# When the four weight sums of a seven-product block are formed: together, or one with each product

## The chip, the cores and the metric

The kernel runs on one core of one Trainium2 chip. Its time is the device time in microseconds (us) of one execution; of several runs the median counts. One more execution was profiled: it gives the trace and the profile page that the text reads.

## The reference

One layer of a streaming encoder on 2048 tokens with 1024 features: chunked softmax attention with a relative bias, then a SwiGLU feed-forward, each between two RMS norms and with a residual.

```python
h = rms_norm(x, g_pre_mix)
q, k, v = split_heads(h, w_qkv)             # 16 heads of 64
# chunk c of 64 frames reads chunks c-8 .. c
p = softmax(q @ k.T / 8 + bias)
x = x + rms_norm(merge_heads(p @ v) @ w_o, g_post_mix)
h = rms_norm(x, g_pre_ffn)
x = x + rms_norm((silu(h @ w_gate) * (h @ w_up)) @ w_down, g_post_ffn)
```

All in float32; the inner width of the feed-forward is 2816.

## The kernel before

**Matmuls.** Every float32 operand of a dense product is split into a high part (a rounded copy, made by ScalarE) and a low part (the rest, a subtraction on VectorE). A product is three matmuls, high by high, high by low, low by high: lines 199, 200 and 201 in `products`. A weight block of 128 x 1024 is split by `split_part`, ScalarE on line 131 and VectorE on line 132.

**Seven products for eight.** The large dense layers (values, queries and keys, gate and up, down) work on 2 x 2 blocks with seven block products in place of eight. Both sides need sums for that. On the token side `Blocks.build` makes the operands B11, B21, T1, T2, B22, T3 and T4 (the names in `BLOCKS`, in the order of use): line 741 makes the difference for T1, line 720 the three combinations for each slice of T2, line 691 or 357 (ScalarE) the high part and line 692 or 358 (VectorE) the low part. On the weight side the seven factors are A11, A12, S1, S2, S4, S3 and A22, where S1 = A21 + A22, S2 = A11 + S1, S4 = A12 + S2 and S3 = A11 - A22 in the kernel's signs and storage.

**Where the weight sums are made.** The down weights' sums are made by DMA. Those of the others are made once, in the first of the two token groups of 1024 tokens, by `block_items`: four blocks are loaded, each sum is one VectorE instruction of 128 x 1024 (line 902), written over one of the four blocks, and stored to DRAM by a GpSimd-issued DMA (line 903) for the second group. There are 17 such sets: 2 for the values (v), 4 for queries and keys (q), 11 for gate and up (g), 68 sums in all.

**Order of the work.** `Stream` runs the weight items ahead of their use: when a product is taken, the item three products on is made (`make`: split, then sums), and its loads start up to six ahead. So in the middle of a set the sums of the next one are made. The two v sets alternate item by item, and each v name has two weight tiles. In `make`, before the change, with n the name of the item:

```python
if n == ("B11" if early else "B21"):
    sum_("S1", "A21", "A21", "A22")
    sum_("S2", "A11", "A11", "A21")
if n == "B21":
    sum_("S4", "A12", "A12", "A11")
if n == "T2":
    sum_("S3", "A21", "A11", "A22", ALU.subtract)
```

`early` holds for q and g. TensorE's order is that of the program; the order on VectorE, ScalarE, GpSimd and SyncE is set by a scheduler that goes by readiness and by place in the program. All queues run in order.

**Who reads the banks.** In a q or g set a product is 24 matmuls into two PSUM banks, 12 each. T4 adds to the two banks that T3 filled, after VectorE has read each of them (the closing: line 1289 in q, 1009 in g). In the v stage a product is 48 matmuls; VectorE adds pairs of products on line 1225, and ScalarE scales the values on line 429.

**Beside the v stage.** The row sums of squares come from token-major copies of x, loaded one after the other into one buffer and squared on ScalarE (line 1344); after four of them VectorE (line 1348) and GpSimd (line 1349) make the roots that line 429 needs.

Of the kernel before, what the change touches and what calls it, by code (L numbers as in the profile page):

```python
# [13 lines left out]
ALU = mybir.AluOpType  # L14
# [24 lines left out]
BLOCKS = ("B11", "B21", "T1", "T2", "B22", "T3", "T4")  # L39
# [10 lines left out]
def trunk(  # L50
# [74 lines left out]
    def w_tile(name):  # L125

        t = wp.tile([P, 2, 1024], F32R, tag="w", name=f"w_{name}", bufs=4)
        return Parts(t)

    def split_part(hi, lo, raw):  # L130
        act.activation(hi, raw, AF.Copy)  # L131
        dve.tensor_tensor(lo, raw, hi.bitcast(F32), op=ALU.subtract)  # L132
# [694 lines left out]
    def weight_sums():  # L827

        def long(t):
            return t.rearrange("(a b) c -> a (b c)", b=2)

        def copy(to, a):
            with tc.issue_after(last_sp[0].ins):
                last_sp[0] = nc.sync.dma_start(long(to), long(a), max_dma_last_dim=8192)

        def add(to, a):
            with tc.issue_after(last_pool[0].ins):  # L840
                pool.dma_start(long(to), long(a), accum_op=ALU.add, max_dma_last_dim=8192)

        steps = [[] for _ in range(4 * len(units) + 16)]
        for u, (src, dst) in enumerate(units):
            at = 8 * (u // 2) + u % 2
            for n, (to, a) in enumerate((("S1", "A21"), ("S3", "A11"), ("S2", "A11"), ("S4", "A12"))):
                steps[at + 2 * n].append((copy, dst[to], src[a]))
            for n, to, a in ((2, "S1", src["A22"]), (4, "S2", dst["S1"]), (5, "S3", src["A21"]), (7, "S4", dst["S2"])):
                steps[at + 2 * n].append((add, dst[to], a))
        for step in steps:  # L850
            yield [f(to, a) for f, to, a in step]
# [39 lines left out]
    def block_items(src, key, early=True, ahead=None):  # L891

        r = {}
        sums_d[key] = {a: dram.tile([P, 1024], F32, name=f"s_{key}_{a}") for a in ("S1", "S2", "S3", "S4")}

        def fetch_(names):
            for a in names:
                r[a] = phase["fp"].tile([P, 1024], F32, tag="w4", name="raw4", bufs=phase["w4"])
                sp.dma_start(r[a], src[BLOCK_AT[a]])

        def sum_(name, to, a, b, op=ALU.add):
            dve.tensor_tensor(r[to], r[a], r[b], op=op)
            last_pool[0] = pool.dma_start(sums_d[key][name], r[to])

        def make(n):
            w = w_tile(f"w{key}_{n}")
            a = FACTOR[n]
            split_part(*w, r[{"S1": "A21", "S2": "A11", "S4": "A12", "S3": "A21"}.get(a, a)])
            if n == ("B11" if early else "B21"):
                sum_("S1", "A21", "A21", "A22")  # L910
                sum_("S2", "A11", "A11", "A21")
            if n == "B21":
                sum_("S4", "A12", "A12", "A11")
            if n == "T2":
                sum_("S3", "A21", "A11", "A22", ALU.subtract)
            return w

        at = {"B11": ("A11", "A12"), "B21": ("A21", "A22")}
        if not early:
            at = {"B11": ("A11",), "B21": ("A12",), "T1": ("A21", "A22")}  # L920
        ahead = ahead or {}
        return [
            (lambda n=n: fetch_(at.get(n, ())), lambda _, n=n: make(n), *ahead.get(n, (6, 3))) for n in BLOCKS
        ]

# [606 lines left out]
    sums_, done = weight_sums(), 0.0  # L1532
# [43 lines left out]
    for t in range(slots):  # L1576
        share = left[0] / max(per - t % per - 1, 1)
        if t > 0 and t % 4 == 0:
            fill(0.5 * share)
            low = jobs[t // 4 - 1].output()  # L1580
            if t % per == 0:
                low()
                low = lambda: None
                n = t // per - 1
# [118 lines left out]
```

## Time and profile before

| | us |
|---|---|
| three runs | 2394.34, 2396.64, 2397.82 |
| median | 2396.64 |
| profiled execution | 2394.31 |
| its span, first to last instruction | 2392.5 |
| TensorE busy | 2342.1 |
| VectorE busy | 1635.7 |
| ScalarE busy | 1147.5 |
| GpSimd busy | 315.6 |
| mean granted TensorE clock | 0.993 |

The profile's engines are PE (TensorE matmuls), PEld (its weight loads), DVE (VectorE), ACT (ScalarE), POOL (GpSimd) and SP (SyncE, which here only issues DMAs). A row of instructions in order of time has the start, the duration, the engine, the line, the operation, what is written from what, the number merged into the row, and in brackets how long the engine stood idle before it and what ended that. Durations of instructions that follow each other overlap a little, so what one costs its engine is the distance from its start to the next one's. Matmuls above all are pipelined: their duration is 0.39 us, their distance smaller.

The rough course of the 2392.5 us: first group's values up to about 97 us, then its queries and keys, the second group's from about 250 us, attention from about 490 us, gate and up of the first group from about 1100 us, then its down projection and the second group's feed-forward.

### The profile page before, as it was taken

Reading aid. Unit: us, or ns where it says so; the run is one execution under the profiler, and the core shown is the slowest. Engines: PE = TensorE matmul, PEld = TensorE weight load, DVE = VectorE, ACT = ScalarE, POOL = GpSimd, SP = SyncE. Lnnn points to the kernel's source line nnn. Section 1 sums busy time; section 2 is a strip of 40 time slices with the busy share of each in tenths; the row PEclk is TensorE's granted clock in tenths of the full one; section 3 lists DMA queues with packets and bytes.
Section 4 is the critical chain, followed back from the end, with each engine's and each line's share of the span. In section 5 each row is a group of like instructions: output and inputs, shape, how many; then the busy total and the mean of one; then the engine's idle time right before and its main releaser. Section 6 shows DMA issues by size and latency. Waiting matters only on the chain.

```text
span 2392.5 us, 32966 instructions
## 1 busy us (share of the span) xinstructions
PE 2342.1 (98%) x11456; PEld 1866.1 (78%) x11456; DVE 1635.7 (68%) x2618; ACT 1147.5 (48%) x2015; POOL 315.6 (13%) x422
## 2 busy tenths in 40 slices
PE   8999999989999999999999999999999999999998
PEld 6877888866666776678888888888888888888887
DVE  7776956666566666659877777677657676545577
ACT  6543643357666666656333332365433333334454
POOL 1022010034324434320000000000000000000001
PEclk9999999999999999999999999999999999999999
DMA  8799988677568977836676553577666657447664
GB/s 304 252 296 325 296 269 256 181 222 223 175 207 254 270 215 231 254 137 208 237 246 206 185 186 129 177 235 258 209 210 207 216 158 238 148 151 249 193 193 145
DMA packets 234966, 523.42 MB, mean 219 GB/s; under 512 B 26896, under 2 KB 43296, under 8 KB 230320
## 3 DMA queue, kind: packets, MB, share of 16 engines
q1 hardware_dynamic: 222896, 474.13, 61.0%
q0 software_dynamic: 11904, 47.19, 6.7%
q8 instruction: 90, 1.47, 0.3%
q14 instruction: 76, 0.62, 0.1%
HBM read 373.85 MB, written 170.44 MB: 227 GB/s over the span
## 4 chain that ended last, share of the span: by engine, by line
PE 56%; DVE 3%; DMA 1%; issue 1%; ACT 0%; SPq 0%; POOL 0%; DVEq 0%; ACTq 0%
PE pd L201 6%; PE pd L199 6%; PE pd L200 6%; PE pb L199 4%; PE pb L201 4%; PE pb L200 4%; PE pa L199 3%; PE pa L201 3%; PE pa L200 3%; PE pc L199 3%; PE pc L201 3%; PE pc L200 3%; PE tt L595 1%; PE tt L565 1%; PE tt L199 1%
## 5 line engine op out<-in xcount | busy, mean ns | idle before, releaser
L550 POOL TENSOR_SCALAR sc<-sc,rows 128x640 f32<-128x640 f32 (+4 forms) x256 | 194.6, 773 | 338.1 <-DVE rows L547 245.5
L538 ACT ACTIVATE sc<-sc,rows 128x640 f32<-128x640 f32 (+4 forms) x256 | 193.0, 756 | 75.1 <-DVE rows L534 74.5
L534 DVE CUSTOM_DVE_ANT_0 sc<-st,bias 128x640 f32<-128x640 f32 (+2 forms) x248 | 174.4, 734 | 53.8 <-issue 26.7
L199 PE MATMUL pb<-hb,w_wg_T 128*128 128x512 f32 x528 | 206.2, 390 | 4.2 <-DVE terms L1009 4.2
L201 PE MATMUL pb<-hb,w_wg_T 128*128 128x512 f32 x528 | 205.5, 389 | 0.0
L200 PE MATMUL pb<-hb,w_wg_T 128*128 128x512 f32 x528 | 205.5, 389 | 0.0
L568 DVE COPY pT<-tt 128x512 f32<-128x512 f32 (+3 forms) x128 | 81.7, 639 | 89.0 <-PE tt L565 67.8
L201 PE MATMUL pd<-a,w_d_T 128*128 128x512 f32 (+1 forms) x368 | 139.9, 380 | 0.1
L199 PE MATMUL pd<-a,w_d_T 128*128 128x512 f32 (+1 forms) x368 | 139.9, 380 | 0.0
L200 PE MATMUL pd<-a,w_d_T 128*128 128x512 f32 (+1 forms) x368 | 139.8, 380 | 0.0
L199 PE MATMUL pa<-hb,w_wg_B 128*128 128x512 f32 x352 | 136.9, 389 | 0.0
L200 PE MATMUL pa<-hb,w_wg_B 128*128 128x512 f32 x352 | 136.9, 389 | 0.0
L201 PE MATMUL pa<-hb,w_wg_B 128*128 128x512 f32 x352 | 136.9, 389 | 0.0
L565 PEld LDWEIGHTS tt<-ident,sc 128*128 128x128 f32 x928 | 106.2, 141 | 35.4 <-issue 14.0
L131 ACT ACTIVATE w_wg_T<-raw 128x1024 fp32r<-128x1024 f32 x88 | 93.0, 1058 | 78.8 <-PE pb L201 33.9
L565 PE MATMUL tt<-ident,sc 128*128 128x128 f32 x928 | 126.0, 276 | 4.1 <-ACT pT L580 4.0
L1011 ACT ACTIVATE terms<-terms 128x512 f32<-128x512 f32 x65 | 41.0, 631 | 173.9 <-DVE terms L1009 173.7
L132 DVE TENSOR_TENSOR w_wg_B<-raw,w_wg_B 128x1024 fp32r<-128x1024 f32 x66 | 80.7, 1223 | 63.4 <-ACT w_wg_B L131 63.3
L291 POOL TENSOR_TENSOR rs<-ms,neg_half 128x4 f32<-128x4 f32 (+1 forms) x7 | 7.5, 1066 | 856.5 <-DVE ms L289 856.5
L358 DVE TENSOR_TENSOR a<-raw_a,a 128x512 fp32r<-128x512 f32 x154 | 105.8, 693 | 21.2 <-ACT a L357 20.6
L199 PEld LDWEIGHTS pb<-hb,w_wg_T 128*128 128x128 f32 x528 | 99.1, 188 | 26.8 <-ACT w_wg_T L131 1.9
L595 PE MATMUL tt<-pT,v 128*64 128x512 f32 (+3 forms) x832 | 119.1, 436 | 0.1
(281 smaller groups left out, 6125.4 us busy)
## 6 DMA issues: line engine op xcount, KB each, us to landing
raw<-in_w_gu SPq DMA_DIRECT2D x77, 512.0 KB, 4.1
k<-k SPq DMA_DIRECT2D x54, 512.0 KB, 6.9
q<-q SPq DMA_DIRECT2D x93, 256.0 KB, 4.7
s_g_S<-raw POOLq DMA_DIRECT2D x44, 512.0 KB, 3.1
raw_d<-d_S SPq DMA_DIRECT2D x88, 256.0 KB, 3.6
raw_a<-aT SPq DMA_DIRECT2D x88, 256.0 KB, 3.7
raw<-s_g_S SPq DMA_DIRECT2D x44, 512.0 KB, 4.0
bias<-ext_d SPq DMA_DIRECT2D x124, 144.0 KB, 6.9
```

Of the source, the lines that this page charges most:

```text
L131: act.activation(hi, raw, AF.Copy)
L132: dve.tensor_tensor(lo, raw, hi.bitcast(F32), op=ALU.subtract)
L199: pe.matmul(pt, a_hi, b_hi, start=first, stop=False, skip_group_check=go_on)
L200: pe.matmul(pt, a_hi, b_lo, start=False, stop=False, skip_group_check=go_on)
L201: pe.matmul(pt, a_lo, b_hi, start=False, stop=last, skip_group_check=go_on)
L358: eng.tensor_tensor(lo, src, hi.bitcast(F32), op=ALU.subtract)
L534: dve.tensor_tensor_reduce(out=sc[:, :n], in0=st[:, c0 : c0 + n], in1=rev, scale=-1.0, scalar=3.0e38, op0=ALU.add, op1=ALU.min, accum_out= ...
L538: act.activation(sc[:, :n], sc[:, :n], AF.Exp, bias=nmax, scale=-1.0, accum_out=rows[:, h : h + 1])
L550: last_pool[0] = pool.tensor_scalar(sc[:, :n], sc[:, :n], rows[:, 2 + h : 3 + h], 1.0, op0=ALU.mult, op1=ALU.mult)
L565: pe.transpose(tt[:, u, :], sc[h][:, b * P : b * P + P], ident)
L568: dve.tensor_copy(dst, tt[:, : len(part), :])
L595: pe.matmul(po[heads[h], c0:c1], v[:, kb, c : c + 64], self.pT[:, h, r, c0:c1], start=m == 0, stop=m == len(terms) - 1,)
```

## The change

The four sums of a set are no longer made two or three with one item. Each item makes at most one: in q and g B11 makes S1, B21 makes S2, T1 makes S4 and T2 makes S3. In v the same four come one item later, with B21, T1, T2 and B22. So each sum is made at least one item ahead of the one whose factor it is. Blocks, buffers, loads, operations and stores are the same, and so are TensorE's instructions.

```diff
-            if n == ("B11" if early else "B21"):
-                sum_("S1", "A21", "A21", "A22")
-                sum_("S2", "A11", "A11", "A21")
-            if n == "B21":
-                sum_("S4", "A12", "A12", "A11")
-            if n == "T2":
-                sum_("S3", "A21", "A11", "A22", ALU.subtract)
+            done = BLOCKS.index(n) - (not early)
+            if 0 <= done < 4:
+                sum_(*(
+                    ("S1", "A21", "A21", "A22"),
+                    ("S2", "A11", "A11", "A21"),
+                    ("S4", "A12", "A12", "A11"),
+                    ("S3", "A21", "A11", "A22", ALU.subtract),
+                )[done])
             return w
```

The file has one line more, so below this place the changed kernel's line numbers are one higher (1009 becomes 1010, 1289 becomes 1290).

**VectorE in the v stage, from the low part of T1's first weight tile on.** raw_285, 294, 300 and 302 are the blocks A11, A12, A21 and A22 of the first v set, raw_290, 296, 305 and 307 those of the second; hb_5 is T1's operand, hb_6 T2's. Before:

```order
L132 TENSOR_TENSOR w_wv_T_422<-raw_300,w_wv_T_422 128x1024
L902 TENSOR_TENSOR raw_294<-raw_294,raw_285 128x1024
L741 TENSOR_TENSOR hb_1_287<-hb_1_287 128x512 x3
L902 TENSOR_TENSOR raw_305<-raw_305,raw_307 128x1024
L692 SCALAR_TENSOR_TENSOR hb_5_408<-hb_1_287,gt,hb_5_408 128x512
L902 TENSOR_TENSOR raw_290<-raw_290,raw_305 128x1024
L132 TENSOR_TENSOR w_wv_T_425<-raw_305,w_wv_T_425 128x1024
L902 TENSOR_TENSOR raw_296<-raw_296,raw_290 128x1024
L692 SCALAR_TENSOR_TENSOR hb_5_408<-hb_1_287,gt,hb_5_408 128x512
L1225 TENSOR_TENSOR v<-pv,terms 128x512
L692 SCALAR_TENSOR_TENSOR hb_5_408<-hb_1_287,gt,hb_5_408 128x512
L1225 TENSOR_TENSOR v<-pv,terms 128x512
```

Changed, the same stretch:

```order
L132 TENSOR_TENSOR w_wv_T_414<-raw_300,w_wv_T_414 128x1024
L741 TENSOR_TENSOR hb_1_287<-hb_1_287 128x512 x3
L692 SCALAR_TENSOR_TENSOR hb_5_400<-hb_1_287,gt,hb_5_400 128x512
L741 TENSOR_TENSOR hb_1_287<-hb_1_287 128x512
L902 TENSOR_TENSOR raw_305<-raw_305,raw_307 128x1024
L692 SCALAR_TENSOR_TENSOR hb_5_400<-hb_1_287,gt,hb_5_400 128x512
L902 TENSOR_TENSOR raw_290<-raw_290,raw_305 128x1024
L132 TENSOR_TENSOR w_wv_T_419<-raw_305,w_wv_T_419 128x1024
L1226 TENSOR_TENSOR v<-pv,terms 128x512
L692 SCALAR_TENSOR_TENSOR hb_5_400<-hb_1_287,gt,hb_5_400 128x512
L1226 TENSOR_TENSOR v<-pv,terms 128x512
L692 SCALAR_TENSOR_TENSOR hb_5_400<-hb_1_287,gt,hb_5_400 128x512
```

The two sums S4 (into raw_294 and raw_296) have left this stretch, and all four low parts of T1 (L692) now stand in it, where before the fourth came after another L741, L1225 and L720.

**ScalarE in the v stage, from T2's second weight tile on.** hb_6 is T2's operand (its last three high parts are here), terms the squared copies or PSUM copies, w_wv_B B22's weight tile. Before:

```order
L131 ACTIVATE w_wv_T_520<-raw_290 128x1024
L1234 ACTIVATE terms<-pv 128x512
L1344 ACTIVATE terms,ssq<-terms 128x1024
L1234 ACTIVATE terms<-pv 128x512
L357 ACTIVATE hb_6_500<-hb_1_287 128x512
L1344 ACTIVATE terms,ssq<-terms 128x1024
L357 ACTIVATE hb_6_500<-hb_1_287 128x512
L429 ACTIVATE v<-v,hr 128x512 x4
L357 ACTIVATE hb_6_500<-hb_1_287 128x512
```

Changed, from the same tile on:

```order
L131 ACTIVATE w_wv_T_516<-raw_290 128x1024
L1235 ACTIVATE terms<-pv 128x512
L1345 ACTIVATE terms,ssq<-terms 128x1024
L357 ACTIVATE hb_6_496<-hb_1_287 128x512
L1235 ACTIVATE terms<-pv 128x512
L357 ACTIVATE hb_6_496<-hb_1_287 128x512
L1235 ACTIVATE terms<-pv 128x512
L1345 ACTIVATE terms,ssq<-terms 128x1024
L131 ACTIVATE w_wv_B_604<-raw_294 128x1024
L357 ACTIVATE hb_6_496<-hb_1_287 128x512
L429 ACTIVATE v<-v,hr 128x512 x4
```

The last high part of T2 now stands before the four scalings of v (L429) and behind the split of a B22 weight tile; the second of the squares has moved ahead of T2's second weight tile, out of this piece.

**VectorE in gate and up, around the closing of T3's first bank.** raw_11022 is A12 of the next set, which the sum S4 overwrites; the set's S1 and S2 stand a few rows above the stretch in both orders. It begins with the second closing of B22 (pc); the next reading of pb is the closing of T3's first bank. Before:

```order
L1009 TENSOR_TENSOR terms<-pc,terms 128x512
L980 TENSOR_TENSOR terms<-terms 128x512
L132 TENSOR_TENSOR w_wg_B_11182<-raw_11022,w_wg_B_11182 128x1024
L1020 TENSOR_TENSOR T_11179<-b_11039,terms 128x512
L902 TENSOR_TENSOR raw_11022<-raw_11022,raw_11020 128x1024
L1009 TENSOR_TENSOR terms<-pb,terms 128x512
```

Changed, the same stretch:

```order
L1010 TENSOR_TENSOR terms<-pc,terms 128x512
L981 TENSOR_TENSOR terms<-terms 128x512
L132 TENSOR_TENSOR w_wg_B_11180<-raw_11022,w_wg_B_11180 128x1024
L1021 TENSOR_TENSOR T_11177<-b_11039,terms 128x512
L1010 TENSOR_TENSOR terms<-pb,terms 128x512
L902 TENSOR_TENSOR raw_11022<-raw_11022,raw_11020 128x1024
```

S4 has changed places with the closing of T3's first bank. The same exchange is found in all three q sets in which a next set is made, and in most of the g sets.

## The prediction

> **What bounds the kernel now.** I read the page first, then TensorE's waits, then tables of windows, then the instructions in order of time around each gap. The page's first part, three of the windows (the columns are span, PE, PEld, DVE, ACT, POOL, then granted clock, DMA share and GB/s) and three of TensorE's waits (total, times, longest):
>
> ```profile
> PE 2342.1 (98%) x11456; PEld 1866.1 (78%) x11456; DVE 1635.7 (68%) x2618; ACT 1147.5 (48%) x2015; POOL 315.6 (13%) x422
> ...
> 30.00:35.00 5.00, 2.85 (x11) 1.43 (x9) 5.00 (x9) 4.42 (x8) 0.65 (x2) 1.00 0.87 264
> 50.00:55.00 5.00, 2.75 (x6) 1.81 (x7) 4.20 (x8) 4.64 (x9) 0.00 (x0) 0.50 1.03 411
> ...
> 300.00:400.00 100.00, 100.00 (x443) 82.84 (x442) 61.43 (x80) 41.96 (x55) 10.85 (x14) 1.00 0.87 264
> ...
> PE pb L199 <- DVE terms L1009: 4.2, 5, 1.5
> PE pb L199 <- DVE terms L1289: 3.9, 3, 2.1
> PE pv L199 <- ACT hb L357: 2.3, 2, 2.0
> ```
>
> TensorE is busy 98% of 2392.5 us, so the change can only win back part of the idle 50 us and of the time at a lowered clock. Its arithmetic is the same before and after: 68 sums, 68 stores, every matmul. What it can change is what stands in front of a waited-for instruction on VectorE. The gaps that sums can touch are in three places: the value stage of the first token group (v), the query and key stage of that group (q), and gate/up of that group (g). In v, VectorE is full (5.00 of 5.00) just when TensorE runs dry, and the granted clock falls to 0.50.
>
> **The v stage, T1.** Rows of TensorE, VectorE and ScalarE in order of time (start, duration, engine, line, what waited):
>
> ```profile
> 29.66 0.39 PE L199 MATMUL pv<-w_wv_T,hb 128*128 128x512 f32 x1
> 45.88 0.39 PE L199 MATMUL pv<-w_wv_T,hb 128*128 128x512 f32 x1
> 53.05 0.79 PE L199 MATMUL pv<-w_wv_T,hb 128*128 128x512 f32 x1 [1.95 <-ACT hb L357]
> 63.70 0.39 PE L199 MATMUL pv<-w_wv_B,hb 128*128 128x512 f32 x1
> ...
> 33.08 0.68 DVE L741 TENSOR_TENSOR hb<-hb 128x512 f32<-128x512 f32 x1
> 33.68 0.69 DVE L1225 TENSOR_TENSOR v<-pv,terms 128x512 f32<-128x512 f32 x1
> 34.94 0.75 DVE L692 SCALAR_TENSOR_TENSOR hb<-hb,gt,hb 128x512 fp32r<-128x512 f32 x1
> ...
> 29.87 1.05 ACT L1344 ACTIVATE terms<-terms 128x1024 f32<-128x1024 f32 x1
> 36.98 1.06 ACT L1344 ACTIVATE terms<-terms 128x1024 f32<-128x1024 f32 x1 [2.46 <-DMA terms<-in_xt]
> 41.73 1.06 ACT L1344 ACTIVATE terms<-terms 128x1024 f32<-128x1024 f32 x1 [0.69 <-DMA terms<-in_xt]
> 46.97 1.06 ACT L1344 ACTIVATE terms<-terms 128x1024 f32<-128x1024 f32 x1 [0.46 <-DMA terms<-in_xt]
> 49.92 2.56 ACT L429 ACTIVATE v<-v,hr 128x512 f32<-128x512 f32 x4 [1.28 <-POOL hr L1349]
> 52.39 0.61 ACT L357 ACTIVATE hb<-hb 128x512 fp32r<-128x512 f32 x1
> ```
>
> The first matmuls of T1, T2 and B22 are at 29.66, 45.88 and 63.70. Undisturbed, a matmul comes every 100 / 443 = 0.226 us (the window from 300), so a v product of 48 takes 10.85 us. T1 loses 45.88 - 29.66 - 10.85 = 5.4 us and T2 17.82 - 10.85 = 7.0 us: 12.4 us, slow clock included. T1 waits for its own operand: the last difference (L741, 33.08) and its low part (L692, 34.94) are late. In the changed order the two S4 sums, one L1225 and one L720 no longer stand ahead of that last L692. One sum and its effect on a q wait:
>
> ```profile
> L902 DVE TENSOR_TENSOR raw<-raw,raw x68: 1212/1218/1229, 18.8 to 1498.5; 128x1024 f32<-128x1024 f32 x68
> ...
> 201.37 1.23 DVE L902 TENSOR_TENSOR raw<-raw,raw 128x1024 f32<-128x1024 f32 x1 [4.29 <-DMA raw<-in_w_qk]
> ...
> 210.57 1.22 DVE L902 TENSOR_TENSOR raw<-raw,raw 128x1024 f32<-128x1024 f32 x1
> 211.71 0.68 DVE L1289 TENSOR_TENSOR terms<-pb,terms 128x512 f32<-128x512 f32 x1
> ...
> 131.50 0.47 PE L199 MATMUL pb<-hb,w_wq_T 128*128 128x512 f32 x1 [1.32 <-DVE terms L1289]
> 171.59 0.47 PE L199 MATMUL pb<-hb,w_wq_T 128*128 128x512 f32 x1 [1.27 <-DVE ms L1348]
> 212.53 0.47 PE L199 MATMUL pb<-hb,w_wq_T 128*128 128x512 f32 x1 [2.12 <-DVE terms L1289]
> 213.79 0.63 PE L201 MATMUL pb<-hb,w_wq_T 128*128 128x512 f32 x1
> 216.78 0.56 PE L199 MATMUL pb<-hb,w_wq_T 128*128 128x512 f32 x1
> ```
>
> From start to start a sum costs VectorE 211.71 - 210.57 = 1.14 us. L692 of the last slice then starts at 34.94 - 2 x 1.14 - (34.94 - 33.68) = 31.4 and ends at 32.15. TensorE needs it with T1's twelfth matmul, 29.66 + 11 x 0.226 = 32.15. T1's 5.4 us go, but for some tenths.
>
> **The v stage, T2: most of that is handed on.** TensorE would now come to T2 at about 40.8 instead of 45.88, before T2's operands exist. These go through ScalarE, which in order also squares the token-major copies of x; each copy is loaded into one buffer, after the square before it. Before, the fourth square starts at 46.97. Four scalings of v stand next, wait 1.28 us for GpSimd and take 2.56, and only then comes the last high part of T2's operand, at 52.39, for which TensorE waits until 53.05. Changed, this high part stands after the fourth square and one half of a weight split (about 1 us), ahead of the scalings. If the fourth square keeps its time, it starts near 46.97 + 1.2 + 1.0 = 49.1, 3.3 us earlier. The first load took 36.98 - 30.92 = 6.1 us from the end of the square before, the next two 3.7 and 4.2; sums were being stored beside the first, and one of those stores now goes later. With about 4 us for each, the fourth square comes at 45.3 and the high part at 47.4, 5.0 us earlier. I take 4.2 us, between the two, and for the range 2.8 (the first square half a microsecond late, the loads as slow as before) up to the whole 12.4. Low clock follows this wait as before, so it cancels. S3 moves behind T2's operands; its only user is T3's split, two products on, so it costs nothing there.
>
> **The q sets.** T4 adds to the banks that T3 filled, after VectorE has read them (L1289, the closing). A product is 24 matmuls, and the first bank must be read within the 12 matmuls of T3's second half, 2.7 us. Before, three sums of the next set (S1, S2, S4) stand ahead of it, and VectorE arrives late: 1.32, 1.27 and 2.12 us. The change puts S4 behind that closing in all three: 3 x 1.14 = 3.4 us, leaving 0.2, 0.1 and 1.0. The clock: after the 2.12 us wait matmuls come 0.43 apart (seven steps from 213.79 to 216.78, 2.99 us instead of 7 x 0.226 = 1.58), 1.4 us lost; after 1.32 and 1.27 there is nothing of the kind. With 1.0 us left I count the 1.4 as gained: q gives 4.8 us, at least 3.4 without the clock.
>
> The Trainium skill ("TensorE: Matmul & The Clock Gate", Part 1, What's actually happening) lets the clock fall to half only after about one idle window of 3.4 us. The trace disagrees at this place: 2.12 us of idleness was enough. By the page the slow matmuls would have another cause and would stay, and the sum would be 1.4 us less.
>
> **The g sets.** The same closing (L1009) in gate/up, all five waits, and VectorE at the second of them:
>
> ```profile
> 1143.17 0.50 PE L199 MATMUL pb<-hb,w_wg_T 128*128 128x512 f32 x1 [0.27 <-DVE terms L1009]
> 1261.00 0.47 PE L199 MATMUL pb<-hb,w_wg_T 128*128 128x512 f32 x1 [1.38 <-DVE terms L1009]
> 1376.79 0.47 PE L199 MATMUL pb<-hb,w_wg_T 128*128 128x512 f32 x1 [0.71 <-DVE terms L1009]
> 1415.45 0.47 PE L199 MATMUL pb<-hb,w_wg_T 128*128 128x512 f32 x1 [0.31 <-DVE terms L1009]
> 1455.75 0.47 PE L199 MATMUL pb<-hb,w_wg_T 128*128 128x512 f32 x1 [1.51 <-DVE terms L1009]
> ...
> 1259.03 1.22 DVE L902 TENSOR_TENSOR raw<-raw,raw 128x1024 f32<-128x1024 f32 x1
> 1260.16 0.68 DVE L1009 TENSOR_TENSOR terms<-pb,terms 128x512 f32<-128x512 f32 x1
> ...
> 1261.42 0.68 DVE L1009 TENSOR_TENSOR terms<-pb,terms 128x512 f32<-128x512 f32 x1
> ```
>
> The changed order puts S4 behind the closing in each. A wait loses up to 1.14 us: 0.27, 1.14 and 0.31 at 1143, 1261 and 1415. At 1376 an operation of 0.60 moves ahead in exchange, so 0.5; at 1455 two more operations move behind, so all 1.5. Together 3.7 us; the low end is 2.5, if two of the smaller waits stay.
>
> **What costs nothing, and its cover.** The 68 stores move with their sums on GpSimd's queue, and some change places with additions into the down weights' sums:
>
> ```profile
> s_g_S<-raw POOLq DMA_DIRECT2D x44, 512.0 KB, 3.1
> ...
> 43.33 2.20 SPq L72 DMA_DIRECT2D raw<-in_w_qk  x2
> ...
> L131 ACT ACTIVATE w_wq_B<-raw x24: 1042/1053/1064, 85.3 to 455.0; 128x1024 fp32r<-128x1024 f32 x24
> ```
>
> A stored sum is read back only in the second token group. What could wait is S3, which overwrites S1's buffer and needs S1's store landed: three products lie between, 16 us, against 3.1 us in flight. If that cover went, VectorE would stop for the rest of the flight. On SyncE's queue the loads of the first query blocks (43.33) slip behind four v stores that wait for the scalings near 50; their first use is the split at 85.3, so some 25 us remain.
>
> **The sum.** 4.2 + 4.8 + 3.7 = 12.7 us of the profiled execution, whose time is 2394.31 (1.8 over its span): 2381.6. The three runs have a median 2.3 us above it, 2396.64, so I predict 2384. A measurement of this kernel can tell about 0.2% from no change, 4.8 us.
>
> **Rivals.**
> - *The forecast holds in all three places* (0.60): v 2.8 to 6, q 3.4 to 4.8, g 2.5 to 3.7: 2382 to 2388.
> - *T2's wait takes back everything in v* (0.16). It is bound by the loads and squares, and TensorE simply waits longer there; for it speaks the 2.46 us at 36.98 that is a DMA's, against it that the last high part leaves the 3.8 us of scalings behind. Then q and g alone: 2396.64 - 8.5 = 2388.
> - *A load takes it back* (0.12). At 201.37 the sum of the fourth q set stopped VectorE for 4.29 us until its block had landed. If that landing keeps its time because the DMA engines are nearly full, all that TensorE won before, 4.2 + 2.3 us, goes into the wait that ended at 212.53, and the slow clock stays. Left are 1.1 there and 3.7 in g: 2392, on the edge of measurable, so half faster, half same. Against it: the load is issued behind k stores that follow TensorE's progress.
> - *Slower* (0.06). The sum that stood before the closing of T3's first bank now stands before that of its second, in 3 q and up to 10 g sets. TensorE needs that one 2.7 us after the first. At 1260.16 and 1261.42 the closings are 1.26 apart; with the sum 2.40, and one more 0.60 operation would make it late. From there each set pays; with a full sum of lateness and a slow clock as at 213.79, 13 x (1.14 + 1.4) = 33 us against 12.7: 2417. It needs 1.4 us in every set to be measurably slower.
> - *No net change* (0.06): VectorE owes the same work, and the waits form again at the next user, 2396.
>
> Faster: 0.60 + 0.16 + 0.06 = 0.82; same 0.06 + 0.06 = 0.12; slower 0.06. The range takes in the first three cases and at its low end v's bound of 12.4: 2384 - 8 = 2376, up to 2392.5; the last two, 0.12, lie outside.
>
> **What would show it.** In the changed trace: T1's first matmul still near 29.7, T2's at 41, B22's near 59.5 (if near 63.7, the second case); the L1289 waits at 0.2, 0.1 and 1.0 us with no 0.43 us spacing behind them; at most one L1009 wait, under 0.5 us; no new wait of T4's second bank. Wrong would be: the sum after the fourth set's load ending no earlier than 202.6, or a closing of the second bank in TensorE's list of waits.

## The result and the profile after

| | before | changed |
|---|---|---|
| median of 12 runs, us | 2393.54 | 2387.83 |
| lowest to highest, us | 2390.53 to 2397.82 | 2383.26 to 2397.90 |
| profiled execution, us | 2394.31 | 2386.56 |
| its span, us | 2392.5 | 2384.8 |

The ratio is 0.9975, with a 95% interval of 0.9965 to 0.9985: a gain of 5.7 us, where the prediction worked out 12.7. A later measurement of the same two kernels (below) gave 8.7.

TensorE's waits in the changed kernel (total, times, longest). The rows for the closing in gate/up, which would now be L1010, are absent; the q stage still has about as much waiting as before (4.8 us beside 5.1, the 3.9 that the list before has for the closing and the 1.27 at 171.59 that it puts down to L1348):

```profile
PE pb L199 <- DVE terms L1290: 4.8, 3, 2.9
PE pv L199 <- ACT hb L357: 4.2, 3, 2.7
PE pv L201 <- DVE hb L358: 0.9, 1, 0.9
```

How far the changed kernel leads at the same matmul (its start before, minus its start after), from the two profiled executions:

| place | before | after | lead |
|---|---|---|---|
| first value product | 7.81 | 8.61 | -0.80 |
| B22 of v | 63.70 | 60.71 | 2.99 |
| row spread in the middle of T3 of v | 81.94 | 80.64 | 1.30 |
| second q set | 137.06 | 134.65 | 2.41 |
| third q set | 177.15 | 177.95 | -0.80 |
| fourth q set | 219.67 | 216.50 | 3.17 |
| second group's values | 258.43 | 256.49 | 1.94 |
| gate/up, early | 1146.71 | 1143.66 | 3.05 |
| gate/up, late | 1461.31 | 1453.58 | 7.73 |

So in these two executions v gave 2.1 us (from -0.80 to 1.30), q 0.6, the stretch from the second group's values through attention 1.1, gate/up 4.7. The parts of v and q went up and down on the way, and that is what the rows show.

**v.** TensorE from T1's first matmul, then VectorE's last low part of T1, then ScalarE:

```profile
30.50 0.39 PE L199 MATMUL pv<-w_wv_T,hb 128*128 128x512 f32 x1
41.38 0.39 PE L199 MATMUL pv<-w_wv_T,hb 128*128 128x512 f32 x1
48.40 0.79 PE L199 MATMUL pv<-w_wv_T,hb 128*128 128x512 f32 x1 [2.69 <-ACT hb L357]
60.71 0.39 PE L199 MATMUL pv<-w_wv_B,hb 128*128 128x512 f32 x1
73.43 0.50 PE L199 MATMUL pv<-w_wv_T,hb 128*128 128x512 f32 x1 [1.22 <-ACT hb L357]
...
31.26 0.75 DVE L692 SCALAR_TENSOR_TENSOR hb<-hb,gt,hb 128x512 fp32r<-128x512 f32 x1
...
45.73 1.06 ACT L1345 ACTIVATE terms<-terms 128x1024 f32<-128x1024 f32 x1 [1.74 <-DMA terms<-in_xt]
47.73 0.61 ACT L357 ACTIVATE hb<-hb 128x512 fp32r<-128x512 f32 x1
69.02 1.06 ACT L1345 ACTIVATE terms<-terms 128x1024 f32<-128x1024 f32 x1 [2.96 <-DMA terms<-in_xt]
71.52 1.34 ACT L429 ACTIVATE v<-v,hr 128x512 f32<-128x512 f32 x2 [0.83 <-POOL hr L1350]
72.77 2.17 ACT L357 ACTIVATE hb<-t 128x512 fp32r<-128x512 f32 x4
```

T1's last low part starts at 31.26 (before 34.94), and T1 takes 41.38 - 30.50 = 10.88 us: its loss of 5.4 us is gone entirely. T2's last high part is at 47.73 (before 52.39), and T2 waits 2.69 us for it. T2 takes 60.71 - 41.38 = 19.33 us, 1.5 more than before. B22 then leads by 3.0, and by 3.8 if one counts that the first product began 0.8 late. But T3 has a new wait, 1.22 us at 73.43. Its four high parts (72.77) now stand behind two scalings, the roots and a square that had waited 2.96 us for its load. Before, the first of these high parts stood ahead of the scalings, and T3 didn't wait:

```profile
71.79 0.63 ACT L357 ACTIVATE hb<-t 128x512 fp32r<-128x512 f32 x1
73.51 1.34 ACT L429 ACTIVATE v<-v,hr 128x512 f32<-128x512 f32 x2 [1.09 <-POOL hr L1349]
```

The loads that these squares wait for are late without a full stage. They go one after the other through one buffer: each leaves when the square before it is done (36.52, 42.01 and 65.03) and lands 3.7 to 4.3 us later. The DMA share of those windows (the last column but one) is far from 1. One load between them, 52.30 to 58.58, ran at 0.97 to 1.00 and took 6.3 us.

```profile
35.00:40.00 5.00, 5.00 (x23) 4.13 (x23) 5.00 (x6) 2.93 (x5) 0.53 (x1) 1.00 0.58 184
40.00:45.00 5.00, 3.96 (x15) 2.28 (x13) 4.78 (x8) 3.16 (x6) 0.53 (x1) 1.00 0.66 230
65.00:70.00 5.00, 5.00 (x23) 4.13 (x22) 3.42 (x5) 2.04 (x5) 0.00 (x0) 1.00 0.43 147
```

**q.** In the changed kernel, the closing's waits in the first, second and fourth set (the third has none), VectorE's split before the second, its idleness before the fourth, and ScalarE's square ahead of that split:

```profile
129.11 0.47 PE L199 MATMUL pb<-hb,w_wq_T 128*128 128x512 f32 x1 [0.24 <-DVE terms L1290]
170.79 0.55 PE L199 MATMUL pb<-hb,w_wq_T 128*128 128x512 f32 x1 [2.87 <-DVE terms L1290]
250.96 0.47 PE L199 MATMUL pb<-hb,w_wq_T 128*128 128x512 f32 x1 [1.66 <-DVE terms L1290]
...
162.50 1.23 DVE L132 TENSOR_TENSOR w_wq_B<-raw,w_wq_B 128x1024 fp32r<-128x1024 f32 x1 [4.73 <-ACT w_wq_B L131]
246.52 0.75 DVE L692 SCALAR_TENSOR_TENSOR hb<-hb,gt,hb 128x512 fp32r<-128x512 f32 x1 [3.03 <-ACT hb L691]
...
160.37 1.06 ACT L1345 ACTIVATE xt<-xt 128x1024 f32<-128x1024 f32 x1 [6.12 <-DMA xt<-in_xt]
```

The same square and split before the change:

```profile
160.28 1.06 ACT L1344 ACTIVATE xt<-xt 128x1024 f32<-128x1024 f32 x1 [3.63 <-DMA xt<-in_xt]
162.42 1.22 DVE L132 TENSOR_TENSOR w_wq_B<-raw,w_wq_B 128x1024 fp32r<-128x1024 f32 x1 [2.25 <-ACT w_wq_B L131]
```

The first and third waits fell from 1.32 and 2.12 to 0.24 and nothing. The second grew from 1.27 to 2.87 and the fourth from 0.42 to 1.66. Before the second, TensorE had come 2.4 us earlier, the square's load had not: it landed at 160.3 in both. ScalarE stood behind it 6.12 us in place of 3.63, the split behind ScalarE, and the closing behind the split. After the wait the clock was at half for 3.7 us (nine matmuls from 170.79 to 174.12, about 0.43 apart).

**Gate/up.** All five waits of the closing, 4.18 us, are gone, and no closing of a second bank has come into the list.

### The profile page after: what moved, and what is told of

Read it like the earlier page. It is cut to its first block, busy times and chain, and to the rows that moved or that the text cites. A ratio compares the mean times of both kernels' runs of the same rounds, so it can differ in the third digit from the quotient of the medians.

```text
span 2384.8 us, 32964 instructions
## 1 busy us (share of the span) xinstructions
PE 2340.3 (98%) x11456; PEld 1866.9 (78%) x11456; DVE 1635.2 (69%) x2618; ACT 1147.6 (48%) x2015; POOL 316.3 (13%) x422
## 4 chain that ended last, share of the span: by engine, by line
PE 61%; DVE 1%; ACT 0%; issue 0%; POOL 0%; DVEq 0%; ACTq 0%
PE pd L201 6%; PE pd L200 6%; PE pd L199 6%; PE pb L199 5%; PE pb L200 5%; PE pb L201 5%; PE pc L199 3%; PE pa L200 3%; PE pc L200 3%; PE pc L201 3%; PE pa L201 3%; PE pa L199 3%; PE tt L595 2%; PE tt L565 1%; PE tt L199 1%; PE st L522 1%
```

## The experiments

Two theories follow from these rows. **Loads:** the sums' new places remove VectorE's lateness as forecast, but in v and q TensorE then meets loads that land when they did before, and the waits form again there. **Plain debt (the rival):** VectorE owes the same work, so it is late again at the next user, whatever the loads do. Both leave nothing of v's and q's gain; the first two experiments test that against a third view, that each part keeps its gain. The medians of the kernel before beside the four groups of runs were 2394.30 (28 runs), 2394.00 (23), 2395.41 (22) and 2393.37 (9).

**1. Each stage's part alone.** The new places for the items of one stage, the old ones for the others:

```diff
+            if key[0] in "v":
                 done = BLOCKS.index(n) - (not early)
...
+            else:
+                if n == ("B11" if early else "B21"):
...
```

> The new places of the sums in the two value sets alone; q and g as before. Both theories expect T2 to begin near 41 and B22 near 60 (before 63.7) in the trace. Loads take it back: the second query set restarts when its block of the token-major copies has landed, near 162.4 whatever TensorE won, so its wait grows from 1.27 to about 3 us and slows the clock; the gain is used up by 180 us and the time is that of before, 0 +- 1.5 us. Each part keeps its gain (rival): about 3 us stay to the end, ratio 0.9987.

> The new places in the four query and key sets alone. Loads take it back: first wait 1.32 to 0.2 us, second stays near 1.2 us (1.1 us won before it, 1.14 us less work ahead of it), third 2.12 to 1 us or less and its slow clock gone; about 3 us in all, ratio 0.9987. Each part keeps its gain (rival): all three waits shrink by 1.14 us and the clock comes back, 4.8 us, ratio 0.998.

> The new places in the eleven gate and up sets alone. Both theories: the five L1009 waits (4.2 us) go, and nothing behind them is bound by a load: 4 to 5 us, ratio 0.998. If the gain of the whole change came from v and q, this one would show none: ratio 1.000.

> The whole change once more beside its parts. Loads take it back: the sum of the three parts, 6 to 8 us, ratio 0.997; in the trace again a wait of 2.5 to 3 us in the second query set near 170 us and one near 250. Rival: 12 us, ratio 0.995.

| new places in | median, us | ratio to before, 95% | waits of the four q sets, profiled execution |
|---|---|---|---|
| v | 2394.23 | 1.0007 (0.9998 to 1.0017) | 0.62, 0.49, 1.88, 0.55 |
| q | 2394.35 | 1.0001 (0.9992 to 1.0009) | 0, 1.99, 0, 1.79 |
| g | 2389.54 | 0.9981 (0.9972 to 0.9990) | 0.85, 2.03, 1.44, 2.34 |
| all (the changed kernel) | 2385.60 | 0.9967 (0.9956 to 0.9979) | 0.64, 2.10, 1.38, 2.38 |

Gate/up alone brings 4.8 us; v alone and q alone bring nothing that these runs can tell, where 4.2 and 4.8 were predicted. The whole brought 8.7 this time, but its interval reaches from 5 to 10.5 us and overlaps that of g alone.

The traces do not show how the gain of v is lost. The expectation for v had the second wait grow to about 3 us; it was 0.49. That profiled execution, 2389.45 us, was the fastest of its eleven, and in it TensorE still led by 3.35 us at the second group's values. So the expectation is right in its time and, as far as this execution shows, wrong in its mechanism. For q it is wrong in its time (about 3 us were expected): with the new places in q alone the first and third wait are gone, but in the whole they are 0.64 and 1.38, about what they are with the old places in q (0.62 in the run of v alone, 1.44 in that of g alone).

**2. v and q together, without gate/up**, the condition above with "vq":

> The new places of the sums in v and q, the old ones in gate and up. Alone, v gave 2394.2 us and q 2394.4 beside 2394.3 of the kernel before. If what v and q win is taken back by loads whatever the other does, the time stays at 2393 to 2395 and the whole change is worth only its gate-and-up part. The rival: the two need each other (the whole change was measured at 2385.6 and its gate-and-up part at 2389.5, so 4 us are unexplained); then this kernel comes to 2390 to 2391.

Measured: 2394.55 us, ratio 0.9999 (0.9989 to 1.0009). Waits of q: 0, 1.55, 0, 2.57. So v and q don't need each other: together they are worth at most 2.6 us, where the forecast had 9.0, and the first expectation holds. Here too the profiled execution (2389.01 us) was the fastest, of twelve, with a lead of 4.9 us at the second group's values. It is the medians that say that nothing is left, and no trace shows where it goes.

**3. Without the second group's squares.** The squares of 160 us are those of the second token group. Their loads, the squares and their buffers are left out, in the changed kernel and in the kernel before:

```diff
             def load(b):
...
+                if n > 1:
+                    return
...
             def use(b):
+                if n > 1:
+                    return
```

> The changed kernel without the second token group's eight token-major loads, their squares on ScalarE and the buffers that they take from the weight blocks (the second group's roots are made from the first group's, so its values are wrong). Theory, loads: the second and fourth waits of the query stage (2.87 and 1.66 us in the changed kernel) hang on these loads; they fall to 0.5 us or less, without a lowered clock behind them, and the time is 4 to 7 us under the changed kernel's 2386 to 2388. Rival, VectorE is late with its own work, sums included: the waits stay between 1 and 3 us and the time is within 2 us of the changed kernel's.

> The kernel before without the same loads, squares and buffers. Theory, loads: the sums still stand ahead of the closing, so the waits of the query stage stay at 1 to 2 us each, the kernel gains at most 3 us, and the distance to the changed kernel without these loads grows from 6 to 8 us to 9 to 12. Rival: the distance stays at 6 to 8.

Measured: changed 2382.92 us (0.9958, 0.9946 to 0.9970), before 2394.02 (0.9995, 0.9986 to 1.0004). The waits of q are 0, 0, 0, 2.32 in the first and 0.64, 0.67, 0, 2.11 in the second. VectorE's split and the fourth closing in the changed kernel without these loads:

```profile
159.97 1.23 DVE L132 TENSOR_TENSOR w_wq_B<-raw,w_wq_B 128x1024 fp32r<-128x1024 f32 x1 [0.46 <-ACT w_wq_B L131]
...
249.19 0.47 PE L199 MATMUL pb<-hb,w_wq_T 128*128 128x512 f32 x1 [2.32 <-DVE terms L1290]
```

The split is 2.5 us earlier than 162.50, although nothing of the sums' work is less, and the second wait is gone. So the 2.5 us were the square's load, or the buffers that these loads take from the weight blocks, for the run leaves out both. TensorE also came to this set 1.7 us later here (lead 0.67 against 2.41), which shortens the wait as well. In the kernel before the expectation missed: its waits were to stay at 1 to 2 us each, and in the profiled execution (2388.42 us, the fastest of eleven) the first three fell to 0.67 or less, while the median stayed. The distance between old and new places is 11.1 us here, as the load theory said, though by the ratios (0.0037, with half widths of 0.0012 and 0.0009, so about 0.0015 to either side) it isn't cleanly apart from the 5.7 to 8.7 with the loads. The fourth wait did not fall: there the theory of these particular loads failed. What VectorE stands behind at 246.52 in the changed kernel is the high part of the second group's operand, and that waits for x itself: ScalarE had stood idle 6.18 us for its load.

**4. One load for the first token half's four squares.** Does T2's wait hang on the loads between the squares?

```diff
-                sp.dma_start(c[b], xt[4 * n + b])
+                if n > 0 or b == 0:
+                    sp.dma_start(c[b], xt[4 * n + b])
```

> The changed kernel; of the first token half's four token-major loads only the first is made and that copy is squared four times (so the scaling of the values is wrong; all four squares stay on ScalarE). Theory, T2's last high part stands behind squares that wait for loads one after the other: without them T2's wait of 2.69 us at 48.40 falls under 0.8 us, its slow clock goes, and B22 begins at 56 to 58 instead of 60.7. Rival, T2's operand is bound by VectorE's own work or by the block loads: the wait stays over 2 us and B22 at 60 to 61. For the whole time the theory that later loads bound the query stage expects nothing to be left of it: 2385 to 2388; the rival there 2382 to 2384.

Measured: 2384.87 us (0.9965, 0.9953 to 0.9977). T2's wait is longer, and ScalarE, one row above its last high part, again waits for a load:

```profile
49.28 0.80 PE L199 MATMUL pv<-w_wv_T,hb 128*128 128x512 f32 x1 [3.88 <-ACT hb L357]
...
47.56 1.06 ACT L1346 ACTIVATE terms<-terms 128x1024 f32<-128x1024 f32 x1 [1.72 <-DMA terms<-in_xt]
```

The expectation missed. With the first four squares out of the way, those of the second 512 tokens moved up in ScalarE's order, and the first load of those took the place. So this run does not say what T2 would wait for without any load. It does show something at T3: its wait near 73 is gone. The last squares are done earlier there, and T3's high parts come at 71.10.

**5. Moving the squares.** Three kernels. In the first the second group's squares are used three steps behind their loads, so that in ScalarE's order they no longer hold the split of B22. In the second the last four begin a set later. In the third the first group's last four squares begin later, so that T3's first high part precedes the scalings:

```diff
-            lag = 0 if room else 1
+            lag = 0 if room else 3
```

> The changed kernel; the second token group's squares are used three steps behind their loads in place of one, so in the second query set ScalarE's split of B22's weight block (L131) no longer stands behind a square that waits for its load. Theory, squares that wait for loads hold the split and so VectorE's closing: the second wait of the query stage (2.87, 2.10, 1.99, 1.55 and 2.81 us in the five traces with the new places in q) falls to 0.6 us or less and the first and third stay at 0 to 0.9; the time falls by 1 to 3 us, to 2384 to 2386. Rival, the loads are late for DMA reasons whoever waits for them (the weight blocks of the next set then come later too): the wait is still over 1.5 us there or turns up in the next set, and the time does not change.

```diff
-pause(8.0) + roots_by_tokens(3, 10.0, 12.0)
+pause(50.0) + roots_by_tokens(3, 10.0, 12.0)
```

> The changed kernel with the loads and squares of the last 512 tokens begun later, in the third query set in place of the second. Theory, it is those squares: the second wait falls to 0.5 us or less and the third set, where the changed kernel waits 0 to 1.4, gets a wait of 1.5 to 3 us; the time stays within 2 us of the changed kernel's. Rival, the second set waits for something else (its own weight blocks, VectorE's work): it still waits 1.5 us or more.

```diff
-(45.0, roots_by_tokens(1, 1.0, 40.0, spare))
+(50.0, roots_by_tokens(1, 1.0, 40.0, spare))
```

> The changed kernel with the first group's second four token-major loads begun a little later in the value stage; in ScalarE's order the first high part of T3's operand then stands ahead of the two scalings that wait for the roots. Theory, the value stage gives back what it wins to these squares and scalings at T3 (waits of 1.22 to 2.31 us near 73 in all five traces with the new places in v, and none where three of the loads were left out): that wait falls under 0.5 us and the whole time by 1 to 2 us. Rival, T3's operand hangs on VectorE or on the weight blocks: the wait stays over 1 us and the time does not move.

| | median, us | ratio to before, 95% | waits of the four q sets |
|---|---|---|---|
| squares behind the split | 2387.93 | 0.9969 (0.9957 to 0.9980) | 0, 0.21, 3.18, 0.88 |
| squares one set later | 2392.26 | 0.9986 (0.9978 to 0.9995) | 0, 1.45, 0.78 and 0.48, 4.10 |
| values' squares later | 2391.81 | 0.9985 (0.9976 to 0.9994) | 0, 2.62, 0, 1.46 |

The first one's third set, TensorE and VectorE:

```profile
211.76 0.76 PE L199 MATMUL pb<-hb,w_wq_T 128*128 128x512 f32 x1 [3.18 <-DVE terms L1290]
...
202.59 1.23 DVE L902 TENSOR_TENSOR raw<-raw,raw 128x1024 f32<-128x1024 f32 x1 [4.63 <-DMA raw<-in_w_qk]
```

The second set's wait fell to 0.21, as expected, and a wait of 3.18 us appeared in the next, as the rival there said: now a sum stands 4.63 us behind the load of its own block, the row that the prediction's third rival was about. Nothing is won. In the second kernel the second set still waited 1.45 us, now for a high part of ScalarE (L439), the wait that grew was the fourth, 4.10, and not the third, and the gain is 3.2 us, less than the changed kernel's: its expectation missed too. The third kernel missed:

```profile
70.46 1.06 ACT L1345 ACTIVATE terms<-terms 128x1024 f32<-128x1024 f32 x1 [3.54 <-DMA terms<-in_xt]
72.16 0.63 ACT L357 ACTIVATE hb<-t 128x512 fp32r<-128x512 f32 x1
73.91 1.33 ACT L429 ACTIVATE v<-v,hr 128x512 f32<-128x512 f32 x2 [1.11 <-POOL hr L1350]
```

T3's first high part now does stand ahead of the scalings, but behind the last square, and that waits 3.54 us for its load: 1.57 us at 72.84, and a second wait of 1.68 at 75.81 for the high parts behind the scalings. Whichever load is put in the place, the wait is there. In v the loads share the one buffer, and the DMA share is only 0.55 from 65 to 70 us in this run.

**6. Less traffic in the stage.** The DMA share in the query stage of the changed kernel (columns as in the prediction's windows; the share is the last but one):

```profile
135.00:155.00 20.00, 20.00 (x92) 16.57 (x91) 14.29 (x19) 9.34 (x13) 5.17 (x7) 1.00 1.03 294
165.00:175.00 10.00, 7.13 (x25) 5.39 (x24) 9.87 (x14) 4.83 (x7) 2.81 (x4) 0.83 0.94 289
175.00:195.00 20.00, 20.00 (x90) 16.55 (x89) 12.86 (x18) 8.41 (x13) 5.06 (x6) 1.00 1.01 311
195.00:215.00 20.00, 20.00 (x92) 16.57 (x91) 16.77 (x21) 6.96 (x10) 4.26 (x6) 1.00 0.99 327
```

The engines are full, or nearly so (0.89 in the window left out, 155 to 165). The Trainium skill ("DMA: Bandwidth & Descriptors", Specifications) gives about 358 GB/s of HBM for one core; windows here with a share near 1 move 294 to 327, so the stage is near that figure without reaching it. It is no ceiling for a window: the prediction's 50 to 55 us moved 411. Part of that traffic is for nobody in this stage: the down weights' sums, made by DMA from 88 us on and used only in the down projections. The edit begins them later, at 350 by the loop's own count, and leaves the rest to the attention. In the trace the first now leaves at 258.5 us and 69 of the 88 before 450, so they are out of the first group's query stage, but most run beside the second group's values and queries:

```diff
-        if 110.0 < done and not 285.0 < done < 350.0 and done % 8.0 < 1.0:
+        if 350.0 < done and done % 8.0 < 1.0:
...
+        if t % 3 == 2:
+            next(sums_, None)
         if t == 16:
             fetch()
```

> The changed kernel; the DMAs that form the down weights' sums begin at 350 us and go on through the attention, in place of beginning near 88 us, so none of them runs in the first group's query stage (there they are 32 KB-row copies between DRAM buffers of 256 KB each, and nothing waits for them). Theory, the query stage's DMA engines are full (0.94 to 1.03 of each window from 135 to 235 us), so loads land late and whatever stands first behind one gives back what the sums' new places win: without this traffic the DMA share there falls under 0.9, the four waits together from 4.8 (6.5 in the second execution) to under 2.5 us, and the time by 2 to 5 us, to 2383 to 2386 where the kernel before gives 2394 to 2395. Rival, the loads are late because they are issued late, behind stores on SyncE's queue or for want of a free buffer: the four waits stay at 4 to 6 us and the time within 1.5 us of the changed kernel's.

Measured: 2381.38 us, ratio 0.9947 (0.9933 to 0.9960), 12.0 us under the kernel before and the best of all, better than the expected 2383 to 2386. Its interval still touches that of the whole in experiment 1. The same windows there:

```profile
135.00:155.00 20.00, 20.00 (x92) 16.57 (x91) 12.14 (x17) 11.75 (x19) 0.53 (x1) 1.00 0.85 272
165.00:175.00 10.00, 10.00 (x46) 8.29 (x45) 10.00 (x14) 3.34 (x5) 0.92 (x2) 1.00 0.72 234
175.00:195.00 20.00, 20.00 (x90) 16.57 (x89) 13.39 (x17) 8.27 (x12) 0.73 (x2) 1.00 0.80 259
195.00:215.00 20.00, 20.00 (x92) 16.57 (x91) 17.75 (x24) 7.44 (x10) 1.60 (x3) 1.00 0.58 193
```

and its waits of TensorE, in which no closing of the q stage (L1290) is left, nor the slow clock behind one; v's are longer than in the changed kernel, 6.2 us against 4.2:

```profile
PE st L522 <- DVE rows L534: 12.6, 29, 2.6
PE pv L199 <- ACT hb L357: 6.2, 3, 2.7
PE tt L199 <- DVE hb L602: 5.8, 5, 2.5
PE tt L565 <- ACT pT L580: 4.0, 4, 1.3
PE prs L353 <- POOL rs L291: 1.5, 1, 1.5
PE warm L1322 <- POOL ident masks.py:199: 1.4, 1, 1.4
PE pb L199 <- DVE terms L1010: 1.1, 1, 1.1
```

All q waits are gone, the fourth with them, and TensorE is busy without a gap from 95 to 255, although one window (215 to 235) still has a DMA share of 0.97. The loads of the second group's x take 7.5 us from issue to landing there, against 10.1 in the changed kernel (median of four of 1024 KB, 95 to 255 us). The lead at the second group's values is 7.6 us, against 1.94. So in this trace the waits of q go with this traffic. How it made the loads late is not settled. The rival, loads issued late behind stores on SyncE's queue, had forecast waits of 4 to 6 us and failed in that. But half of the moved DMAs are issued by SyncE itself (line 837, 21 of them between 95 and 255 us in the changed kernel), so the run shortened SyncE's queue as well as unloading the engines, and changed its order. The load that the second set had waited for left at 139.11 in place of 153.56 and landed at 144.78 in place of 160.26: 14.5 us were won at the issue and 1.0 in flight. The two are linked. From 95 to 255 us SyncE never has more than eight DMAs in flight in the changed kernel, and its issues at 144.19, 148.20 and 149.79 come within 0.06 us of the landing of the one eight places before. Slow flights there hold up later issues.

What stays open besides: the old places of the sums were not run with the down sums moved, so how much of the 12.0 us needs the sums' new places is not measured. And the profiled execution is the slowest of the five (2386.89; the others 2380.53 to 2383.15). In attention its lead falls from 8.6 to 3.0, with a wait of 2.15 us for VectorE at 597.02 and slow matmuls behind it and near 680. Whether the moved DMAs have a part in that, and whether the other executions lose it too, was not seen.

## Why the prediction was right, and where not

The direction was right and the measured 2387.83 lies inside the likeliest case's 2382 to 2388, but that case did not happen as it was put: it wanted all three places to hold, and one did. That the number fell there is luck in part. The 2384 was the median of three runs, 2396.64, less 12.7; twelve runs gave 2393.54, from which 12.7 would have led to 2380.8. The gain was 5.7 to 8.7 us, and by the medians of experiments 1 and 2 the terms for v and q were not in it.

- **T1's 5.4 us go: right.** T1 takes 10.88 us, what 48 undisturbed matmuls take.
- **T2's wait takes most of it back: right, with the size a little off.** The fourth square came at 45.73 and the high part at 47.73, where the loads played forward gave 45.3 and 47.4. B22 leads by 3.8 counted from its own start, forecast 4.2; it began at 60.71 and not near 63.7, so the second rival, that T2's wait takes back everything in v, did not happen. "Low clock follows this wait as before, so it cancels" was wrong: 0.43 us and more between matmuls lasts from 48.40 to 55.01, 6.6 us, against 3.6 before. At half speed that is 1.5 us more lost.
- **After v: not foreseen.** The prediction's working for v ended at B22. ScalarE's order also changed one product on, at T3, and 1.7 us went back there (lead 2.99 to 1.30). By the medians the new places in v alone are worth between 0.5 us won and 4.1 lost, so of the predicted 4.2 more is missing than T3 took; where it goes stays open. In all eight traces with the new places in v and the first group's loads as they were T3 waits, 1.22 to 2.51 us; in the four with the old places it waits once, 0.62.
- **q, 4.8 us: the term that failed.** The step "3 x 1.14 = 3.4 us, leaving 0.2, 0.1 and 1.0" holds for the first and third set: 0.24 and none. It fails for the second, 2.87 in place of 0.1, and the fourth rose from 0.42 to 1.66. The prediction counted each wait by what VectorE does just ahead of it, and the second was put down to a sum where, once the sum had gone, a load was late next. The third rival, a load that takes it back, is what the trace of the changed kernel shows at the second and fourth set. I gave it 0.12 and looked for it one set too late: the sum at 201.37 that it named waits 2.67 us in the changed kernel and does no harm, and experiment 5 brings the harm about. Its ground against, that the load is issued behind stores that follow TensorE's progress, was right for the issue and wrong for the landing: the copies for the squares were issued 2.3 us earlier (153.56, before 155.89) and landed at the same time.
- **Gate/up, 3.7 us: right, and a little more.** 4.7 in the two traces, 4.8 alone by the medians, which is most of the change's whole worth. The DMA share there is 0.65 from 1100 to 1300. The share alone does not decide it: v's loads were late at 0.43 to 0.66, and from 255 to 350 us the changed kernel has a share of 0.90 and no wait of TensorE.
- **The slower rival** did not come: the closing of the second bank, 2.7 us later, is not in the changed kernel's list of waits. It is once elsewhere, 0.48 us at 212.01 with the squares a set later.
- **No net change, for VectorE owes the same work:** for v and q the medians came out as it said. Its ground, VectorE's own work, does not account for q's waits: in experiment 6 VectorE has the same instructions and q has no wait.

Single traces mislead by more than a term's size here: the executions that were profiled of the changed kernel ended q with a lead of 1.94 and of -2.71, and its gate/up part won 4.7 and 4.6 in both. Only the medians say that v and q are worth nothing by themselves.

## What to carry to other kernels

Removing work from in front of a waited-for instruction pays where the next thing behind it has slack. In gate/up all of it stayed. In v and q a load was next in whichever place the order put one, so ask of each wait which load will be late once the work is gone, and whether that load is held by its buffer, by its queue or by the DMA engines. The DMA share alone does not tell: loads were late in v at 0.43 to 0.66 and in q at 0.89 to 1.03. Where a stage is nearly full, look for traffic that nobody in it needs; with it moved, q's waits were gone.

## What was not expected of the hardware

Half clock follows some waits and not others of the same length. It came after 1.95 us (at 53.05, before), 2.31 us (at 74.20, without the second group's squares) and 2.87 us (at 170.79); it did not come after 2.32 us at 249.19 in that same kernel, nor after 2.62 us in the second q set of the values' later squares. After the 4.10 us wait at 252.24 four matmuls ran at full speed, and only then 0.43 us apart, from 253.24 to 256.63. The stretches at 170.79 and 253.24 last 3.7 and 3.4 us, one after a wait of 3.18 us (211.76, squares behind the split) 5.7. The Trainium skill ("TensorE: Matmul & The Clock Gate", Part 1, What's actually happening) speaks of a free-running window of about 3.4 us, in which an idle one drops the clock and a busy one restores it. The late start behind 252.24 and two of the three lengths agree with that. That a whole such window must be idle does not agree: 1.95 us was enough.
